# The order of the filler work and of four loads in the loop of a hybrid attention step

## The chip, the core and the metric

The program runs on one core of one Trainium2 chip. Its time is the device time of one execution in microseconds (us); the lower, the better. A core has TensorE (matrix products, rows PE and, for the loading of weights, PEld), VectorE (DVE), ScalarE (ACT), GpSimd (POOL) and SyncE (SP). In this program all transfers are issued by SyncE, in the order in which they were written down.

## What is computed

One layer of a decoder with two attention mixers side by side, for 2048 prompt positions and 8 sample tokens, in 32-bit floats:

```python
h = einsum('bsd,de->bse', x, w_in)            # 1024 -> qA,kA,vA,gA, qB,kB,vB,gB
# mixer A: 8 heads, three banded patterns with strides 1, 4, 16, merged by their maxima and denominators
# mixer B: 8 query heads on 2 key/value heads, one banded pattern, a learned sink per head
mix = concatenate([oa * silu(ga), ob * silu(gb)], axis=-1)     # 512 + 512 = 1024 rows
out = einsum('bse,ed->bsd', mix, w_o)                          # 1024 x 1024
y = layer_norm(ALPHA * x + out)
```

Every band has 128 positions behind each query and is worked in blocks of 128 queries with 128 or 256 keys. The keys and values are outputs as well.

## The kernel before

**Stages.** Four stages follow one another: the projection of keys, queries and some of the rest (0 to 240 us in the profile); the projection of values, with mixer A's sample tokens woven in (to 380 us); the attention loop (380 to about 1045 us); the output projection with the layer norm (to the end). A product of two 32-bit matrices is made of three products of split operands (high by high, high by low, low by high), so each weight tile is first split: VectorE copies it rounded ("h", L137), GpSimd subtracts to get the rest ("l", L138).

**The attention loop** (from L1113) runs over 16 jobs of 4 groups, 64 rounds, and two more rounds in which the last groups drain. A job is a head pair with one stride: rounds 0 to 47 are mixer A's four pairs with strides 16, 4 and 1; rounds 48 to 63 are mixer B's four pairs, four rounds each (rounds 48, 52, 56, 60). In a round TensorE computes scores of the new group (L823), turns the exponentials of the group before (transposes, L853) and multiplies the turned ones of the group before that with the values (L874). VectorE adds the mask and finds the extremes (L831), and copies the turned tiles out of PSUM (L859); ScalarE takes exponentials (L834). `fetch_q` (L800) reorders on VectorE the queries of the next group. A round has four steps; all engines execute in the order that is written (`manual_schedule`).

**Filler.** At each step `advance(RATE / 4)` lets a generator issue other products, charged with their columns divided by 2.4 per ns, until RATE / 4 = 3650 / 4 ns are spent; a yield of None ends the step. The filler is first `stream` (L568): the projection of 11 more tiles of 128 columns (three of B's queries, eight gates) in three passes of 4, 4 and 3 tiles; a pass goes over eight chunks of 256 positions, a tile and a chunk take 24 products (L628, tile `pg`), 2112 products in all. At the switch of passes the weights change: in the last chunk of a pass `Parts` puts four parts for each new tile in a list. `raw_step`, called at each step, loads parts into four buffers (`raw`, L142) and splits loaded parts, first in first out, two a step at most, if their tile has its place (`open`) and three steps have passed since the load was issued. A place can be opened only when the old tile in it is done; before the change `pend` opens it after the 24 products of the next tile.

**Head of the output projection.** After the stream, `out_weights` (L714) loads the last weights of the output projection (rows 2 and 3; rows 0 and 1 were put in the list in the last chunk, rows 5, 6, 4, 7 by `late_wo` in rounds 53, 57, 58, 59), waits until B's first two pairs are merged, and makes for three blocks of 128 positions the products with rows 0 to 5 of the eight row tiles (0 to 3 are mixer A's, 4 to 7 are B's four pairs): 3 x 6 x 2 x 3 = 108 products of 512 columns (L672). What is not done when the loop ends is issued right behind it.

**Merging.** When a pair of A is done, `merge_a` fetches weights F from DRAM for eight pieces (L1038), GpSimd multiplies and adds (L1050 to L1053), and the result goes to `ms`. `merge_b` does the like in three pieces (L951 to L997). These run in a queue of chains, one yield a step.

**Loads.** `loads` (L1084) issues the keys and queries of the next pair: for A in rounds 5 and 8 of a pair, for B in rounds 1 (keys) and 2 (queries) of the pair before.

**Last stage** (from L1161): first the sample tokens (L162), then the 16 blocks; a block that was begun in the loop lacks rows 6 and 7 (12 products), any other all eight (48 products).

Of the kernel before, what the change touches and what calls it, by code (L numbers as in the profile page):

```python
# [36 lines left out]
RATE = 3650  # L37
# [6 lines left out]
AHEAD = 3  # L44
# [7 lines left out]
def hymba_step(ctx, tc, xt, xs, xr, wq, wv, wo, tab, msk, ident, diag, sinks, lng, lnb,  # L52
# [513 lines left out]
    def stream(passes):  # L566

        with tc.tile_pool(name="gw", bufs=1, side="right", reuse_waits="tile") as gw, \  # L568
# [25 lines left out]
            def first_wo(i):  # L594
                t = kept.tile([128, 2, 8, 128], F32R, name="wo%d" % i, tag="w%d" % i)
                wo_parts[i].open((t[:, 0], t[:, 1]))

            nxt, pend = X5, []
# [4 lines left out]
            for pi, names in enumerate(passes):  # L603
# [7 lines left out]
                for c, c2 in zip(route, route[1:] + [None]):  # L611
                    c0 = 256 * c
                    n = TOK - c0 if c == 7 else 256
                    x, nxt = nxt, []
                    if c2 is None:
                        for name in more:
                            ws[name] = Parts(wq[TILES.index(name)])
                        if not more:
                            wo_parts.update((i, Parts(wo[:, i].rearrange("p (a b) -> p a b", b=128))) for i in range(2))
                    for i, name in enumerate(names):  # L620
                        p = ps.tile([128, 512], F32, name="pg", tag="mm", bufs=2)
                        wh, wl = ws[name]
                        for kt in range(8):
                            if c2 is not None and kt % 2 == 0 and i == 1:
                                nxt.append(piece(c2, len(nxt)))
                            xh, xl = x[kt // 2]
                            for e, (a, b) in enumerate(((wh, xh), (wh, xl), (wl, xh))):
                                T.matmul(p[:, :n], a[:, kt, :], b[:, kt % 2, :n], start=kt + e == 0, stop=kt == 7 and e == 2)  # L628
                                yield n / 2.4
                        EMIT[name[0]](go, XC, p[:, :n], name, c0, n)  # L630
                        if name[0] == "Q":
                            queries.append(name)
                        if news:
                            next(news, None)
                        for fn in pend:
                            fn()
                        pend = []
                        if c2 is None:
                            if not more and i < 2:
                                pend.append(lambda i=i: first_wo(i))  # L640
                            for e in range(i, len(more) if name == names[-1] else min(i + 1, len(more))):
                                pend.append(lambda e=e, name=more[e]: weights(e, name))
                nxt = x
            for fn in pend:
                fn()
# [6 lines left out]
    def mixed(pool, tb, kts, z, bufs, hbufs, here=None):  # L652

        nk = len(kts)
        h, l, t, g = [pool.tile([128, nk, 128], d, name="m" + a + z, bufs=n) for a, d, n in zip("hltg", (F32R, F32R, F32, F32), (hbufs, hbufs, bufs, bufs))]
# [48 lines left out]

    def late_wo(kt):

        pool, tag, bufs = {4: (ot, "oT2", 1), 5: (kp, "v", 2), 6: (kp, "k", 2), 7: (kp, "q", 2)}[kt]
        t = pool.tile([128, 2, 8, 128], F32R, name="wl%d" % kt, tag=tag, bufs=bufs)
        out_parts(kt, (t[:, 0], t[:, 1]))

    def out_weights():
        wO = wscope.enter_context(tc.tile_pool(name="wO", bufs=1, side="right", reuse_waits="tile"))
        for kt in (2, 3):
            out_parts(kt, [wO.tile([128, 8, 128], F32R, name="wo%d%s" % (kt, a)) for a in "hl"])  # L714
            yield None
            yield None
        while len(merged) < 2:
            yield None
        oh = wscope.enter_context(tc.tile_pool(name="oh", bufs=1, side="right", reuse_waits="tile"))
        xs_ = [oh.tile([128, D], F32, name="xh%d" % tb) for tb in range(AHEAD)]  # L720
        for tb, x in enumerate(xs_):
            dma(x, xr[tb * 128:tb * 128 + 128])
        kts = (0, 1, 2, 3, 5, 4)

        def gated(tb):
            cols = slice(tb * 128, tb * 128 + 128)
            t, g = [kept.tile([128, 6, 128], F32, name="h" + a, tag="p%d" % i) for i, a in enumerate("tg")]
            dma(g, gs[0:6, :, cols].rearrange("k p t -> p k t"))
            dma(t, ms[0:6, :, cols].rearrange("k p t -> p k t"))
            return t, g  # L730

        nxt = gated(0)
        first.clear()
        for tb, x in enumerate(xs_):
            t, g = nxt
            for _ in range(5 if tb == 0 else 3):
                yield None
            h, l = [oh.tile([128, 6, 128], F32R, name="h" + a, tag="h" + a) if tb % 2 else kept.tile([128, 6, 128], F32R, name="h" + a, tag="p%d" % (i + 2))
                    for i, a in enumerate("hl")]
            V.tensor_mul(t, t, g)  # L740
            split(h, l, t, V)
# [3 lines left out]
            for nh in range(2):  # L745
                p = ps.tile([128, 512], F32, name="po", tag="mm", bufs=2)
                yield from out_products(p, {kt: (h[:, kt], l[:, kt]) for kt in kts}, nh, True, True)
                xx = x[:, nh * 512:nh * 512 + 512]
                V.scalar_tensor_tensor(xx, xx, ALPHA, p, op0=OP.mult, op1=OP.add)
            first[tb] = x  # L750
# [334 lines left out]
    for before, p in zip(pairs, pairs[1:]):  # L1085
        s0 = starts[pairs.index(before)]
        loads[s0 + (1 if before.isb else 5)] = p, "k"
        loads[s0 + (2 if before.isb else 8)] = p, "q"
    spare = {starts[5] + 1: 5, starts[6] + 1: 6, starts[6] + 2: 4, starts[6] + 3: 7}
# [25 lines left out]
    with tc.manual_schedule(engines=set(ENGINES)):  # L1115
# [5 lines left out]
        for i in range(N + 2):  # L1121
# [16 lines left out]
            for sl in range(4):  # L1138
# [7 lines left out]
                advance(RATE / 4)  # L1146
# [16 lines left out]
    with tc.tile_pool(name="ol", bufs=1, reuse_waits="tile") as ol:  # L1163
# [7 lines left out]
        for i, tb in enumerate([16] + list(range(16))):  # L1171
# [3 lines left out]
            if tb in first:  # L1175
                x, m = first[tb], {}
# [5 lines left out]
            if tb < 16:  # L1182
                m.update(mixed(ol, tb, range(6, 8), "p", 2, 3, resident[-2:]))
# [151 lines left out]
```

## Time and profile before

| | us |
|---|---|
| median of 3 runs (lowest to highest) | 1236.95 (1236.46 to 1239.42) |
| the profiled execution: its own time | 1242.7 |
| the profiled execution: span from first to last instruction | 1240.9 |
| TensorE busy (matrix products) | 1149.8 |
| VectorE, ScalarE, GpSimd busy | 569.6, 430.5, 331.6 |
| mean granted TensorE clock | 0.972 |

Rows of the views by time read: start in us from the beginning of the span, duration, engine, line, operation, output<-inputs, shapes, count, and in square brackets how long the engine had been idle before and what released it. A view by windows gives for each stretch its length and then the busy time of PE, PEld, DVE, ACT and POOL with counts, the granted clock, the share of the DMA engines and GB/s. Products are pipelined: a row of n products lasts n spacings and a tail of some 0.2 us. A round begins where its sixteen score products (L823) begin.

### The profile page before, as it was taken

What the parts mean: (1) busy time and instruction counts of PE and PEld (TensorE: products, weight loads), DVE (VectorE), ACT (ScalarE), POOL (GpSimd) and SP (SyncE); (2) the same over time, 40 slices, a digit from 0 to 9 for tenths busy, and PEclk for the clock granted to TensorE, in tenths of its full rate; (3) what the DMA queues carried; (4) which work ended last, traced back from release to release, by engine and by line L of the source; (5) the groups of instructions that cost most, each with busy time, mean ns of one, the idle gap of its engine ahead of it and who ended that gap; (6) DMA issues with size and microseconds to landing.
All of it is one profiled execution on the core that took longest, in us unless ns stands there. A gap on an engine that the chain in (4) does not pass through costs nothing.

```text
span 1240.9 us, 23423 instructions
## 1 busy us (share of the span) xinstructions
PE 1149.8 (93%) x8614; PEld 1010.2 (81%) x8614; DVE 569.6 (46%) x1849; ACT 430.5 (35%) x1414; POOL 331.6 (27%) x400
## 2 busy tenths in 40 slices
PE   7999999999998999997999999699887977999997
PEld 7899999979978888986888788678766855688885
DVE  6522001010024554555665455555555775575544
ACT  3200111101103555554555455345443542132221
POOL 2233102120011000054224204620252332265442
PEclk9999999999999999998999999899998988999999
DMA  8745887293785654676458857676666755935531
GB/s 277 248 134 176 259 270 252 80 284 116 231 253 168 191 161 154 153 186 173 153 159 199 258 146 195 139 193 185 166 171 192 229 182 151 252 106 186 194 131 68
DMA packets 205971, 230.15 MB, mean 185 GB/s; under 512 B 34544, under 2 KB 174480, under 8 KB 205472
## 3 DMA queue, kind: packets, MB, share of 16 engines
q1 hardware_dynamic: 205856, 228.66, 63.2%
q8 instruction: 67, 1.10, 0.4%
q14 instruction: 48, 0.39, 0.1%
HBM read 158.52 MB, written 70.07 MB: 184 GB/s over the span
## 4 chain that ended last, share of the span: by engine, by line
PE 67%; DMA 16%; DVE 6%; ACT 5%; issue 3%; SPq 2%; POOL 1%; DVEq 0%; POOLq 0%; ACTq 0%
PE po L672 14%; PE pg L628 11%; PE pv L527 8%; DMA F<-fd 6%; PE ps_s L823 6%; PE ps_pt L853 5%; PE ppt L152 5%; PE pmm L152 5%; PE ps L152 5%; PE ps_o L874 4%; ACT pe L834 4%; PE po L152 3%; DVE pT L859 2%; DMA gx<-xd 2%; DMA raw<-in_wq 1%
## 5 line engine op out<-in xcount | busy, mean ns | idle before, releaser
L834 ACT ACTIVATE pe<-sm,st 128x256 f32<-128x256 f32 (+1 forms) x512 | 235.6, 461 | 228.1 <-DVE st L831 227.2
L831 DVE CUSTOM_DVE_ANT_0 sm<-ps_s,mk 128x256 f32<-128x256 f32 (+1 forms) x512 | 180.4, 375 | 139.5 <-PE ps_s L823 128.8
L853 PE MATMUL ps_pt<-idt,pe 128*128 128x128 f32 x848 | 141.2, 288 | 51.7 <-DVE pT L859 51.4
L628 PE MATMUL pg<-gx,gw 128*128 128x256 f32 (+1 forms) x1104 | 165.3, 293 | 8.3 <-DMA gx<-xd 2.9
L853 PEld LDWEIGHTS ps_pt<-idt,pe 128*128 128x128 f32 x848 | 94.0, 143 | 74.4 <-DVE pT L859 60.5
L628 PEld LDWEIGHTS pg<-gx,gw 128*128 128x128 f32 x1104 | 142.2, 192 | 9.7 <-issue 4.5
L859 DVE COPY pT<-ps_pt 128x512 f32<-128x512 f32 x176 | 121.2, 689 | 29.0 <-PE ps_pt L853 26.2
L1050 POOL TENSOR_TENSOR oT<-oT,F 128x256 f32<-128x256 f32 x32 | 23.5, 736 | 355.2 <-DMA F<-fd 256.8
L874 PE MATMUL ps_o<-pT,v 128*64 128x128 f32 (+1 forms) x1120 | 107.8, 337 | 0.0
L874 PEld LDWEIGHTS ps_o<-pT,v 128*64 128x64 f32 x1120 | 70.6, 138 | 40.3 <-issue 17.9
L834 ACT ACTIVATION_READ_ACCUMULATOR pe<-sm,st 128x1 f32 x512 | 95.8, 187 | 0.0
L823 PE MATMUL ps_s<-k,qo 64*128 64x256 f32 (+1 forms) x768 | 95.1, 389 | 0.0
L823 PEld LDWEIGHTS ps_s<-k,qo 64*128 64x128 f32 x768 | 68.9, 194 | 13.6 <-issue 2.2
L628 PE MATMUL pg<-gx,gw2h 128*128 128x256 f32 (+1 forms) x368 | 75.5, 293 | 1.2 <-ACT spe L406 1.2
L527 PE MATMUL pv<-wvh,xl 128*128 128x384 f32 (+1 forms) x224 | 70.3, 314 | 0.0
L527 PE MATMUL pv<-wvh,xh 128*128 128x384 f32 (+1 forms) x224 | 70.2, 313 | 0.0
L527 PE MATMUL pv<-wvl,xh 128*128 128x384 f32 (+1 forms) x224 | 70.1, 313 | 0.0
L628 PEld LDWEIGHTS pg<-gx,gw2h 128*128 128x128 f32 x368 | 58.8, 192 | 1.6 <-ACT spe L406 1.5
L628 PE MATMUL pg<-gx,gw2l 128*128 128x256 f32 (+1 forms) x184 | 54.1, 294 | 0.0
L539 ACT ACTIVATE vf<-pv 128x384 f32<-128x384 f32 (+1 forms) x32 | 14.0, 437 | 113.3 <-PE pv L527 67.3
L857 ACT ACTIVATE pT<-ps_pt 128x256 f32<-128x256 f32 (+1 forms) x48 | 23.6, 491 | 81.7 <-PE ps_pt L853 81.6
L628 PE MATMUL pg<-gx,gw3h 128*128 128x256 f32 (+1 forms) x240 | 49.9, 296 | 0.0
(278 smaller groups left out, 2485.7 us busy)
## 6 DMA issues: line engine op xcount, KB each, us to landing
gx<-xd SPq DMA_DIRECT2D x80, 512.0 KB
F<-fd SPq DMA_DIRECT2D x80, 192.0 KB
gs<-th SPq DMA_DIRECT2D x64, 128.0 KB
v<-vs SPq DMA_DIRECT2D x28, 256.0 KB
xo<-in_xr SPq DMA_DIRECT2D x13, 512.0 KB
xd<-xh SPq DMA_DIRECT2D x12, 512.0 KB
xd<-xl SPq DMA_DIRECT2D x12, 512.0 KB
kc<-in_kca SPq DMA_DIRECT2D x8, 768.0 KB
```

The costliest lines, as they stand in the source:

```text
L152: T.matmul(p[:, :n], a[:, kt, :], b, start=k == 0, stop=k == 23)
L527: T.matmul(p[:, :w], l, r[:, kt, :w], start=k == 0, stop=k == 23)
L628: T.matmul(p[:, :n], a[:, kt, :], b[:, kt % 2, :n], start=kt + e == 0, stop=kt == 7 and e == 2)
L672: T.matmul(p, a, b[:, nh * 4:nh * 4 + 4].rearrange("p a b -> p (a b)"), start=first and k == 0, stop=last and k == end)
L823: T.matmul(s[:, h, n % 4, :w], self.Q[g][r, n % 4 * 128:n % 4 * 128 + 128], self.keys(n)[r], start=True, stop=True)
L831: V.tensor_tensor_reduce(sm[:, :w], self.s[:, h, n % 4, :w], mk[:, MI[self.d], 256 - w:], -0.125, 3.0e38, op0=OP.add, op1=OP.min, accum_out=m)
L834: S.activation(p[:, :w], sm[:, :w], AF.Exp, scale=-1.0, bias=m, accum_out=den)
L853: T.transpose(pt[:, h, j], self.P[h, n][:, a:a + 128], idt)
L857: S.activation(t, pt, AF.Copy)
L859: V.tensor_copy(t, pt)
L874: T.matmul(o[64 * h:64 * h + 64, a:a + 128 * len(ns)], v[:, cv, kv:kv + 64], t[:, h, j:j + len(ns)].rearrange("p a b -> p (a b)"), start=n ...
L1050: G.tensor_mul(m, m, F[:, 0])
```

## The change

Nothing is computed otherwise; the order is changed in six places.

- `RATE` falls from 3650 to 3480; in round 0 each step gets `RATE / 2` in place of a quarter.
- The places of new weights are opened one step after the last product that used them (`soon(..., 1)`), no more after the next tile.
- In the loop, the head of the output projection covers four blocks. It begins with rows 0 to 3 for a block with an odd number, or while fewer than two pairs of B are merged; else with rows 0 to 5. The wait for B's first two merges is gone. The first block's inputs are loaded when the last chunk of the stream begins.
- The output weights change places: rows 0, 1, 2, 3 come in rounds 53, 57, 58, 59 (`late_wo`), rows 4 and 5 into the places of the first two gate tiles, rows 6 and 7 at the end of the stream.
- In the last stage a block that was begun with four rows makes up rows 4 and 5; the loads of all blocks' mixed and gate rows go to the places `p0` to `p3`, which the head's tiles also use.
- B's keys are issued in round 0 of the pair before and its queries in round 1.

```diff
-RATE = 3650
+RATE = 3480
-AHEAD = 3
+AHEAD = 4
...
                         if not more:
-                            wo_parts.update((i, Parts(wo[:, i]...)) for i in range(2))
+                            head.append(gated(0))
+                            wo_parts.update((i, Parts(wo[:, i]...)) for i in (4, 5))
...
-                        for fn in pend:
-                            fn()
-                        pend = []
                         if c2 is None:
                             if not more and i < 2:
-                                pend.append(lambda i=i: first_wo(i))
+                                soon(lambda i=i: first_wo(i), 1)
                             for e in range(i, len(more) if name == names[-1] else min(i + 1, len(more))):
-                                pend.append(lambda e=e, name=more[e]: weights(e, name))
+                                soon(lambda e=e, name=more[e]: weights(e, name), 1)
...
+    def gated(tb):
+        n = 6 if len(merged) > 1 and tb % 2 == 0 else 4
+        cols = slice(tb * 128, tb * 128 + 128)
+        t, g = [kept.tile([128, 6, 128], F32, name="h" + a, tag="p%d" % i)[:, :n] for i, a in enumerate("tg")]
+        dma(g, gs[0:n, :, cols].rearrange("k p t -> p k t"))
+        dma(t, ms[0:n, :, cols].rearrange("k p t -> p k t"))
+        return t, g
...
     def late_wo(kt):
-        pool, tag, bufs = {4: (ot, "oT2", 1), 5: (kp, "v", 2), 6: (kp, "k", 2), 7: (kp, "q", 2)}[kt]
+        pool, tag, bufs = {2: (ot, "oT2", 1), 0: (kp, "v", 2), 1: (kp, "k", 2), 3: (kp, "q", 2)}[kt]
...
     def out_weights():
-        for kt in (2, 3):
+        for kt in (6, 7):
             out_parts(kt, [wO.tile([128, 8, 128], F32R, name="wo%d%s" % (kt, a)) for a in "hl"])
             yield None
             yield None
-        while len(merged) < 2:
-            yield None
...
-        nxt = gated(0)
+        nxt = head[0]
         for tb, x in enumerate(xs_):
             t, g = nxt
-            for _ in range(5 if tb == 0 else 3):
+            dma(x, xr[tb * 128:tb * 128 + 128])
+            for _ in range(3 if tb else 1):
                 yield None
...
-        loads[s0 + (1 if before.isb else 5)] = p, "k"
-        loads[s0 + (2 if before.isb else 8)] = p, "q"
-    spare = {starts[5] + 1: 5, starts[6] + 1: 6, starts[6] + 2: 4, starts[6] + 3: 7}
+        loads[s0 + (0 if before.isb else 5)] = p, "k"
+        loads[s0 + (1 if before.isb else 8)] = p, "q"
+    spare = {starts[5] + 1: 0, starts[6] + 1: 1, starts[6] + 2: 2, starts[6] + 3: 3}
...
-                advance(RATE / 4)
+                advance(RATE / 4 if i else RATE / 2)
...
             if tb in first:
-                x, m = first[tb], {}
+                x, n = first[tb]
+                m = mixed(ol, tb, range(n, 6), "o", 2, 2) if n < 6 else {}
...
-                m.update(mixed(ol, tb, range(6, 8), "p", 2, 3, resident[-2:]))
+                m.update(mixed(ol, tb, range(6, 8), "p", 2, 4, resident[-2:]))
```

## What was predicted

> **What bounds the kernel now.** I read the page first, then the busy times by windows. TensorE is busy 93% of the span, so only the rest can be won, and the question is where it lies. One window of the loop in full flow, five others:
>
> ```profile
> 440.00:460.00 20.00, 20.00 (x177) 17.04 (x174) 12.28 (x51) 11.83 (x44) 0.00 (x0) 1.00 0.60 161
> 800.00:820.00 20.00, 13.41 (x93) 11.11 (x95) 10.04 (x33) 5.96 (x21) 11.62 (x19) 0.77 0.57 152
> 920.00:940.00 20.00, 10.86 (x87) 9.47 (x87) 6.18 (x23) 5.62 (x19) 7.61 (x11) 0.83 0.96 243
> 1000.00:1020.00 20.00, 12.64 (x97) 9.86 (x95) 18.09 (x52) 9.64 (x34) 10.68 (x12) 0.85 0.51 165
> 1020.00:1040.00 20.00, 15.64 (x86) 10.06 (x87) 11.01 (x30) 6.67 (x20) 6.88 (x8) 0.76 0.85 240
> 1100.00:1120.00 20.00, 20.00 (x88) 16.24 (x87) 13.25 (x18) 5.34 (x10) 14.04 (x11) 1.00 0.44 150
> ```
>
> At 440 and in the last stage (1100) TensorE has no gap. At 800 and 920 it stands for 7 and 9 us with the clock down, at 1000 VectorE is full (18.09) and TensorE waits, at 1020 it is idle again and slow. The waits, longest first, say what it waits for in the loop:
>
> ```profile
> PE ps_pt L853 <- DVE pT L859: 50.5, 33, 9.1
> ```
>
> Turns wait for VectorE's copies. VectorE executes in order, so the question of each such wait is what stood ahead of the copy. So I read VectorE's and SyncE's timelines at the three bad places.
>
> **The change, part by part.** I number rounds as the kernel part does.
>
> *B's queries one round earlier.* The 9.1 us wait, by the timelines of DVE, PE and SP:
>
> ```profile
> 934.97 0.43 DVE L800 COPY qo<-q 128x512 f32<-128x512 f32 x1 [9.50 <-DMA q<-qb]
> ```
> ```profile
> 936.06 1.11 PE L853 MATMUL ps_pt<-idt,pe 128*128 128x128 f32 x4 [9.14 <-DVE pT L859]
> ```
> ```profile
> 908.66 5.53 SPq L463 DMA_DIRECT2D od<-vsd  x8
> ...
> 920.11 1.35 SPq L906 DMA_DIRECT2D q<-qb  x2
> ```
>
> This is round 55, where `fetch_q` wants B's third pair. Its queries were issued in round 54 (its second step belongs here too: each load is two steps of two DMAs), 920 on SyncE, behind eight small loads of the sample tokens (5.53 us) and the merge's F. They land 15 us later. A round is some 10.5 us (below), so issued in round 53 they stand ahead of those eight loads and land about 10 us before they are needed: the whole 9.14 goes. What is late next is the same queue's F and `gx` (stream) traffic, at a DMA share of 0.96; so I bound the gain from 3 us (that traffic gives most of it back) to 11 (with the slow clock behind the wait, 0.83) and take 9.5. B's other loads (the keys' four DMAs and the other pairs' queries) move past F, `ms` and `raw` issues too; none of them shows a wait, nor do their buffers, whose last reader is a round back: nothing.
>
> *RATE.* The filler costs per product, and a round of B costs, by the chain of work:
>
> ```profile
> 499.04 2.02 PE pg L628 x17
> ...
> 964.34 1.95 PE ps_s L823 x16
> ...
> 974.85 1.95 PE ps_s L823 x16
> ```
>
> 0.119 us a product, 10.5 us a round. The stream is 2112 products charged 226.2 us; at 3.65 a round it ends after 62.0 rounds. At 3.48, with round 0 counted twice, after 64.0. So 65 products (7.0 / 0.107) pass from the rounds before 62 into rounds 62 and 63: 7.7 us leave the earlier part where TensorE is full. Late rounds have small gaps of their own, so I take 6.5 (3 to 7.7).
>
> Round 0 itself gains 30 products in this gap:
>
> ```profile
> 389.35 2.08 PE L823 MATMUL ps_s<-k,q 64*128 64x128 f32 x16 [3.43 <-DVE st L831]
> ```
>
> But the third tile's weights are then needed in round 0 and the fourth's early in round 1, before their splits; they are forced. I take nothing beyond their 3.6 us of work (plus or minus 1.5).
>
> *The end of the loop.* PE's timeline, then DVE's:
>
> ```profile
> 1006.16 2.00 PE L823 MATMUL ps_s<-k,qo 64*128 64x256 f32 x16
> ...
> 1017.72 1.11 PE L853 MATMUL ps_pt<-idt,pe 128*128 128x128 f32 x4 [3.79 <-DVE pT L859]
> 1019.58 0.39 PE L963 MATMUL pst<-idt,wts 128*32 128x128 f32 x1 [0.75 <-ACT pT L857]
> 1019.91 3.79 PE L823 MATMUL ps_s<-k,qo 64*128 64x256 f32 x16
> ...
> 1027.17 0.66 PE L853 MATMUL ps_pt<-idt,pe 128*128 128x128 f32 x4 [0.78 <-DVE pT L859]
> ...
> 1053.47 0.73 PE L672 MATMUL po<-wo,hh 128*128 128x512 f32 x2 [2.52 <-ACT hh L109]
> ...
> 1072.42 0.62 PE L162 MATMUL po<-wo,mixS 128*32 128x512 f32 x1
> ```
> ```profile
> 1004.82 2.20 DVE L137 CAST wo<-raw 128x256 fp32r<-128x256 f32 x2
> ```
>
> Round 62 takes 13.75 us without one filler product, because VectorE splits the four weights that the head needs first. From its start to the sample tokens (1072.42) it is 66.3. After: rows 0 to 3 come by `late_wo` and are split by round 60; the other sixteen parts follow in rounds 62 to 65, as many casts as before, but no head product waits for them before the third block. Rounds 62 and 63 with filler at 10.8 each (0.3 for casts): 21.6. Round 64 has neither filler nor scores: values 1.9 and five turns of 0.66 + 0.78, some casts between: 9.5. Three more for the first block's split (2.52 and its product's start). Then 108 products of the head at 20 / 88 = 0.227: 24.5; it is 108 as before, 4 + 4 + 6 + 4 rows in place of three times 6. Two gaps where a block's split waits for the loads before it: 3 (one is here, 2.52) and 2. Slow clock: 1.5. Sum 65.1 against 66.3: 1.2 gained, while 65 products more are done in it. The round of 64 is my weakest number; the tail can gain 8 (no gaps, full clock) or lose 6 (waits for `raw` as in 1004.82).
>
> On the clock: the scores at 1019.91 take 3.79, those at 1006.16 take 2.00, after a wait of 3.79. The Trainium skill, "TensorE: Matmul & The Clock Gate", Part 1, says that an idle window of some 3.4 us halves the clock until TensorE has been busy as long; the trace agrees, 3.79 against 2.00. By that rule the new tail, with gaps of 0.8 and 2.5, would not slow down at all, and the sum would be 1.5 lower; I keep the 1.5, as the window at 1020 has 0.76.
>
> *Places opened at once.* This speaks against the change. At the first switch of passes, DVE and SP:
>
> ```profile
> 562.29 0.69 DVE L859 COPY pT<-ps_pt 128x512 f32<-128x512 f32 x1
> ...
> 575.71 0.58 DVE L137 CAST gw<-raw 128x256 fp32r<-128x256 f32 x1 [5.56 <-DMA raw<-in_wq]
> ...
> 584.14 0.65 DVE L137 CAST gw<-raw 128x256 fp32r<-128x256 f32 x2 [3.20 <-DMA raw<-in_wq]
> ```
> ```profile
> 569.59 2.00 SPq L142 DMA_DIRECT2D raw<-in_wq  x4
> ```
>
> The first cast stands in round 21, step 0, and waits 5.56 for a part that SyncE could issue only at 569.59, behind the merge's F. When that part lands doesn't depend on the place. A pass of four tiles is charged 82.2 us and so ends at round 22.5 (82.2 / 3.65), after the change at 22.6; its last chunk begins four tiles (10.3 us charged) earlier, at 19.7 in both. The place was opened after two of these tiles, 1.4 rounds on, in round 21; now it is opened after one tile and a step, in round 20, step 1, and the cast stands in step 2: right behind the copy of 562.29, so VectorE waits from about 563 rather than 570.15 and holds its copies, the turns and TensorE 7.2 us longer. The second wait (3.20) then goes, as its part lands meanwhile. So 4 lost (0 to 7.2). At the second switch (DVE, POOL, SP):
>
> ```profile
> 802.73 1.30 DVE L137 CAST gw<-raw 128x256 fp32r<-128x256 f32 x2 [7.25 <-POOL F L1052]
> ```
> ```profile
> 804.63 2.79 POOL L138 TENSOR_TENSOR gw<-raw,gw 128x256 fp32r<-128x256 f32 x4
> ```
> ```profile
> 799.81 6.59 SPq L142 DMA_DIRECT2D raw<-in_wq  x4
> ```
>
> Here the next part waits for a buffer that GpSimd frees only behind the merge of A's third pair. By the same counting the lower RATE puts this switch 1.25 rounds later (45.1 to 46.3). The opening at once takes back most of that: the casts that wait here stood in step 1 of round 44 and now stand in step 3, half a round in which the stall is shorter. But the first tile's subtractions now queue behind the merge's last piece on GpSimd and no more before it, so the buffers come free later. I get 0.5 lost (3 gained to 9 lost).
>
> *Last stage.* Three blocks of 24 products and one of 12 in place of three of 12 and one of 48: 84 either way, then twelve of 48. Their loads wait for places that the head still holds, covered by the fourth block and the sample tokens (5.5 + 7 us): nothing; without that cover 3.
>
> **Sum.** -9.5 - 6.5 - 1.2 + 4 + 0.5 = -12.7, on the profile's span 1240.9: 1228.2. That execution took 1242.7, its median sisters 1236.95; I take the same difference from the median: 1224. What I call no change is within 0.3% (3.7 us), about what a measurement of this kernel can tell.
>
> **Rivals.**
> 1. *The tail closes up.* The tail gains 8, the queries 11, the first switch loses 2: -23, so 1214. For it: the window at 1020 is idle and slow; against: round 64 has nothing to fill its turns. 14%.
> 2. *The queue is the limit.* The queries' stall comes back as waits for F and `gx` (gain 3), and the first switch loses 6: -4.2, so 1233. For it: share 0.96; against: SyncE's 5.53 us now come after the queries. 13%.
> 3. *Slower: casts that stand too early.* At both switches VectorE waits from half a round earlier: 7.2 and 9 lost, with 1.8 of slow scores each; and since these waits end at times that the merges set, the 3 us saved in the rounds just before vanish: -14 + 18 = +4, so 1241. It decides from 14 us lost at the switches. For it: the 5.56 and 7.25 above; against: the part's landing after that serves more casts at once. 10%.
> 4. *No effect*: the loop is bound by the merges' chain of loads throughout. Against: the gapless window at 440. 2%.
>
> **How the numbers follow.** The forecast has 61%, its own range 1215 to 1231. Over 0.3% faster: 61 + 14 + half of rival 2 = 81%; same: the other half and rival 4, 9%; slower 10%. The range from 1211 to 1235 takes in rivals 1 and 2 and leaves out rival 3 and some of the edges.
>
> **What would show it.** No `qo` copy of round 55 waits for `q`; round 55 takes some 11 us. Round 62 holds 33 stream products and takes under 12. Before the first cast of the first switch VectorE waits 10 us or more, in round 20. Head products start with `wo0` right after round 65 begins, with 41 of 108 in the loop's steps, counted as above. I am wrong if the window around round 55 stays as idle as 10.86 of 20, if the switches cost over 14 us more, or if the last stage no longer runs gapless.

## The result, and the profile after

The changed kernel is slower: 1244.12 us median of 5 runs (1241.27 to 1245.74) against 1236.46 (1232.59 to 1239.42) of the kernel before beside it, ratio 1.0066 with a 95% interval of 1.0040 to 1.0093. Its profiled execution took 1243.91 us, span 1242.1. The forecast was 1224, with a range of 1211 to 1235 and 10% on slower.

The profiled execution of before on which the prediction rests was long in its span (1240.9). The kernel before was therefore profiled once more among the experiments: 1236.17 us, span 1234.4. This span and that of the profile after differ by 7.7 us, the two medians by the same, so this second profile of before is the one to set against the profile after. The two profiles of the kernel before differ by 1.3 to 1.6 us in each of the first four stretches below; differences of that size between single profiles say nothing.

I cut both spans where the score products (L823) of a round begin. The rows below are from the view by windows: stretch, length, then busy time of PE, PEld, DVE, ACT, POOL, granted clock, share of the DMA engines, GB/s. The stretches are rounds 21 and 22 (the first switch of passes), 34 and 35, 44 to 46 (the second switch), 54 to 56 (B's third queries), and round 62 to the sample tokens' products (L162). The last stage, from there to the start of its last product, took 159.5 us before and 159.7 after, with TensorE busy all the time. First the kernel before, run again:

```profile
564.61:592.40 27.79, 21.29 (x164) 17.94 (x164) 15.93 (x54) 11.08 (x39) 14.51 (x21) 0.94 0.71 182
693.38:714.85 21.47, 19.92 (x170) 16.90 (x169) 11.35 (x42) 11.19 (x39) 0.00 (x0) 1.00 0.77 243
784.33:824.14 39.81, 30.55 (x242) 25.69 (x241) 21.42 (x75) 16.18 (x58) 16.69 (x29) 0.91 0.72 182
901.97:946.56 44.59, 32.42 (x258) 27.64 (x257) 20.92 (x80) 17.04 (x59) 19.56 (x28) 0.89 0.72 191
999.58:1065.89 66.31, 52.80 (x267) 37.12 (x266) 40.10 (x98) 17.77 (x49) 20.06 (x22) 0.85 0.69 205
```

The same rounds of the changed kernel:

```profile
563.67:599.71 36.04, 22.32 (x160) 18.50 (x159) 16.60 (x56) 11.30 (x39) 17.31 (x25) 0.81 0.63 150
699.24:726.06 26.82, 22.82 (x167) 18.66 (x166) 11.16 (x41) 11.28 (x39) 2.52 (x4) 0.87 0.81 263
795.59:839.58 43.99, 31.83 (x237) 26.18 (x236) 22.21 (x77) 16.39 (x58) 21.72 (x34) 0.88 0.61 155
915.47:948.09 32.62, 30.17 (x267) 25.28 (x266) 21.00 (x79) 16.84 (x59) 16.89 (x25) 1.00 0.71 193
1003.05:1073.37 70.32, 57.81 (x331) 44.20 (x330) 41.03 (x112) 18.79 (x54) 20.92 (x24) 0.90 0.69 205
```

So rounds 54 to 56 win 12.0 us, with the clock full and TensorE busy for 30.2 of 32.6 us; the first switch loses 8.25, rounds 34 and 35 lose 5.35, the second switch 4.2, the end 4.0; the last stage is the same. All other rounds from 0 to 61 together win 2.6 (482.7 against 485.3). The sum is +7.2. Of the 12.0 us, 1.95 come back within that 2.6: rounds 57 to 61 take 55.0 us instead of 53.0, since a wait for the sample tokens' work, 2.3 us in rounds 54 to 56 before, now stands there with 1.4.

The list of TensorE's waits in the changed kernel (total, times, longest) is to be set against 50.6 us, 38 times, longest 8.8, in the kernel before, run again (the 50.5 us that the prediction began with are for the span from 500 us on):

```profile
PE ps_pt L853 <- DVE pT L859: 37.6, 38, 7.2
PE ps_pt L853 <- DVE stT L930: 10.2, 1, 10.2
```

Together 47.8 us, no more than before: by this list alone the change looks harmless. On the two pages TensorE is busy for 1146.8 of 1234.4 us (before, run again) and for 1149.4 of 1242.1 (after), so it stands 5.1 us longer and works 2.6 longer on the same products, at a lower clock in places. The lengths of the rounds tell where.

**The first switch.** VectorE's and SyncE's timelines of the changed kernel, the stretch between the last copy of round 20 and the turns behind it:

```profile
561.51 0.68 DVE L859 COPY pT<-ps_pt 128x512 f32<-128x512 f32 x1
575.37 1.96 DVE L137 CAST gw<-raw 128x256 fp32r<-128x256 f32 x4 [13.18 <-DMA raw<-in_wq]
...
585.23 0.64 DVE L137 CAST gw<-raw 128x256 fp32r<-128x256 f32 x2 [2.55 <-DMA raw<-in_wq]
```
```profile
569.46 1.89 SPq L142 DMA_DIRECT2D raw<-in_wq  x4
```

The parts are issued at 569.46, as before (569.59), and the cast ends its wait at 575.37, as before (575.71; 575.09 in the profile run again). Only the waiting begins earlier: the cast now stands directly behind the copy of 561.51, and VectorE does nothing for 13.18 us, where it did half a round of work before and then waited 5.56 (4.86 in the profile run again). TensorE's timeline shows who pays:

```profile
577.58 1.12 PE L853 MATMUL ps_pt<-idt,pe 128*128 128x128 f32 x4 [10.25 <-DVE stT L930]
```

**B's queries.** The timelines of VectorE and SyncE in the changed kernel, rounds 53 to 55:

```profile
922.34 0.64 DVE L800 COPY qo<-q 128x512 f32<-128x512 f32 x1
```
```profile
913.38 1.86 SPq L906 DMA_DIRECT2D q<-qb  x2
...
918.32 0.34 SPq L581 DMA_DIRECT2D gx<-xd  x1
...
933.06 6.50 SPq L463 DMA_DIRECT2D od<-vsd  x8
```

No copy of queries waits any more, neither this one nor the next at 934.73. Two things have moved: the queries are issued a round earlier, and the eight loads of the sample tokens (`od`), which stood ahead of the queries and of the stream's `gx`, now stand behind both. The second is the work of RATE: these loads are listed with the stream's tiles, and on SyncE they come behind `gx` in the kernels with RATE 3480 and ahead of it in those with 3650.

**The end.** TensorE's and VectorE's timelines of the changed kernel behind the loop:

```profile
1034.56 1.22 PE L672 MATMUL po<-wl,hh 128*128 128x512 f32 x2 [2.33 <-ACT hh L109]
...
1043.98 0.37 PE L963 MATMUL pst<-idt,wts 128*32 128x128 f32 x1 [4.65 <-DVE wts L959]
...
1050.69 0.73 PE L672 MATMUL po<-wl,hh 128*128 128x512 f32 x2 [2.04 <-ACT hh L109]
```
```profile
1037.49 0.29 DVE L137 CAST wo7h<-raw 128x256 fp32r<-128x256 f32 x1 [2.26 <-DMA raw<-in_wo]
...
1041.21 0.69 DVE L137 CAST wo7h<-raw 128x256 fp32r<-128x256 f32 x2 [2.45 <-DMA raw<-in_wo]
```

Two waits of VectorE for output weights 7, which only the last stage reads, stand ahead of the last steps of pair 7's statistics (`wts`); the transpose of these (L963) stands ahead of the head's next products on TensorE.

### The profile page after: what moved, and what is told of

Read it like the earlier page. It is cut to its first block, busy times and chain, and to the rows that moved or that the text cites. A ratio compares the mean times of both kernels' runs of the same rounds, so it can differ in the third digit from the quotient of the medians.

```text
span 1242.1 us, 23436 instructions
## 1 busy us (share of the span) xinstructions
PE 1149.4 (93%) x8614; PEld 1006.3 (81%) x8614; DVE 566.0 (46%) x1855; ACT 430.9 (35%) x1417; POOL 328.6 (26%) x402
## 4 chain that ended last, share of the span: by engine, by line
PE 65%; DMA 13%; DVE 7%; ACT 5%; issue 4%; POOL 3%; SPq 2%; POOLq 0%; DVEq 0%; ACTq 0%
PE po L672 13%; PE pg L629 11%; PE ps_s L823 7%; PE pv L527 7%; PE ps_pt L853 5%; PE pmm L152 5%; PE ps L152 5%; PE ppt L152 4%; ACT pe L834 4%; PE ps_o L874 4%; DMA F<-fd 4%; PE po L152 3%; DVE pT L859 3%; DVE sm L831 2%; DMA k<-ks 2%
## 5 line engine op out<-in xcount | busy, mean ns | idle before, releaser
L853 PEld LDWEIGHTS ps_pt<-idt,pe 128*128 128x128 f32 x848 | 90.7, 141 | 73.3 <-DVE pT L859 48.9
L823 PE MATMUL ps_s<-k,qo 64*128 64x256 f32 (+1 forms) x768 | 95.5, 390 | 0.0
L823 PEld LDWEIGHTS ps_s<-k,qo 64*128 64x128 f32 x768 | 69.3, 195 | 13.4 <-issue 1.8
L527 PE MATMUL pv<-wvl,xh 128*128 128x384 f32 (+1 forms) x224 | 69.4, 310 | 0.0
L672 PE MATMUL po<-wl,mho 128*128 128x512 f32 x192 | 59.7, 392 | 0.0
L172 DVE SCALAR_TENSOR_TENSOR th<-th,pg 128x256 f32<-128x256 f32 (+1 forms) x64 | 26.9, 420 | 48.7 <-ACT th L168 48.3
```

Of the source, the lines that this page charges most:

```text
L172: V.scalar_tensor_tensor(th[:, :n], th[:, :n], 1.0, p, op0=OP.add, op1=OP.mult)
L527: T.matmul(p[:, :w], l, r[:, kt, :w], start=k == 0, stop=k == 23)
L672: T.matmul(p, a, b[:, nh * 4:nh * 4 + 4].rearrange("p a b -> p (a b)"), start=first and k == 0, stop=last and k == end)
L823: T.matmul(s[:, h, n % 4, :w], self.Q[g][r, n % 4 * 128:n % 4 * 128 + 128], self.keys(n)[r], start=True, stop=True)
L853: T.transpose(pt[:, h, j], self.P[h, n][:, a:a + 128], idt)
```

## The experiments

The lengths of the same rounds in all profiles, and the ratios to before of the same job (the letters of the theories are defined anew in each expectation). The lengths are of one profile each, in us:

| kernel | 21, 22 | 34, 35 | 44-46 | 54-56 | 0-61 | 62 to sample | ratio (95%) |
|---|---|---|---|---|---|---|---|
| before (b0) | 27.8 | 21.5 | 39.8 | 44.6 | 619.0 | 66.3 | 0.9989 (0.9962-1.0016) |
| loads | 28.0 | 21.5 | 42.8 | 44.9 | 623.3 | 66.2 | 0.9987 (0.9960-1.0014) |
| RATE | 29.1 | 27.0 | 37.3 | 41.5 | 618.9 | 75.2 | 1.0065 (1.0039-1.0091) |
| places | 35.8 | 21.5 | 41.1 | 44.9 | 629.0 | 68.7 | 1.0061 (1.0031-1.0090) |
| head | 27.6 | 21.5 | 40.9 | 43.5 | 619.9 | 67.1 | 1.0015 (0.9994-1.0036) |
| head, loads | 27.9 | 21.5 | 39.6 | 44.7 | 620.1 | 67.6 | 1.0013 (0.9996-1.0031) |
| head, loads, RATE | 28.4 | 26.2 | 37.4 | 32.6 | 609.2 | 71.8 | 0.9964 (0.9942-0.9985) |
| all four (after) | 36.0 | 26.8 | 44.0 | 32.6 | 622.2 | 70.3 | 1.0066 (1.0040-1.0093) |
| head, RATE, places | 34.2 | 26.0 | 44.6 | 38.5 | 628.1 | 70.8 | 1.0131 (1.0098-1.0164) |
| head, loads, places | 33.1 | 21.5 | 40.7 | 43.5 | 627.4 | 63.5 | 1.0037 (1.0015-1.0060) |

**1. The kernel before, unchanged.**

> The kernel before, unchanged. Theory A (the profiled execution of before, 1242.7 us, was an unusual one, 6 us over the median, because its transfers fell badly): round 55 takes clearly less than the 20.5 us of that profile, and the span is some 1235 us. Theory B (the profile is typical and only the profiling adds time): round 55 takes about 20 us again and the span is about 1240 us.

1236.01 us; round 55 takes 20.2 us in this profile too, as theory B had it, and yet the span is 1234.4, as theory A had it. So the stall of the queries was there in both profiles, and it is not what made the first one long: its 6.5 us more are spread over many rounds.

**2. The loads alone** (before, with `0 if before.isb` and `1 if before.isb` in `loads`).

> The kernel before with B's keys and queries issued one round earlier, nothing else. Theory A (the stall of round 55 is there in few executions): within 3 us of before. Theory B (it is there in each): 9 to 13 us faster. In both, VectorE no longer waits for q in round 55.

1236.12 us, no difference: the time of theory A, but not its reason, as the stall is there again in experiment 1. The wait for `q` is gone, and yet rounds 54 to 56 take 44.9. TensorE waits 5.5 us for `gx` there, and works 35.2 us where it worked 32.4, at a granted clock of 0.85. TensorE's and SyncE's timelines say why:

```profile
928.88 1.65 PE L628 MATMUL pg<-gx,gw 128*128 128x256 f32 x6 [3.34 <-DMA gx<-xd]
```
```profile
908.26 6.05 SPq L463 DMA_DIRECT2D od<-vsd  x8
...
922.09 2.16 SPq L581 DMA_DIRECT2D gx<-xd  x1
```

The stream's next chunk `gx` stood behind the same eight loads and the merge's F. The queries had hidden that it was late as well.

**3. RATE alone** (3480, and round 0 twice).

> The kernel before with RATE 3480 and the doubled first round, nothing else. Theory A (products moved from full rounds to the idle end are won): 4 to 8 us faster. Theory B (they are paid again behind the loop, where the head now starts later): no change, within 3 us.

1245.15 us, slower by itself, which neither theory had. To round 61 it is level (618.9); the end takes 8.9 us longer. TensorE's and VectorE's timelines there:

```profile
1042.43 0.37 PE L963 MATMUL pst<-idt,wts 128*32 128x128 f32 x1 [14.80 <-DVE wts L959]
```
```profile
1039.72 0.64 DVE L137 CAST wo3h<-raw 128x256 fp32r<-128x256 f32 x2 [8.27 <-DMA raw<-in_wo]
```

The stream ends two rounds later, so the head's weights are loaded two rounds later, and their casts come to stand ahead of pair 7's statistics.

**4. The places alone** (`soon(..., 1)` for `pend`).

> The kernel before with the weights' places opened one step after their last use, nothing else. Theory A (the cast stands half a round earlier before a part whose landing the merge sets): 4 to 7 us slower at the first switch of passes, and at the second switch up to 5 us either way. Theory B (the places opened early spread the casts): 1 to 4 us faster.

1245.10 us, slower, and by a little more than theory A had. The first switch takes 35.8 instead of 27.8, the second little more than before. VectorE's timeline:

```profile
573.05 1.96 DVE L137 CAST gw<-raw 128x256 fp32r<-128x256 f32 x4 [11.99 <-DMA raw<-in_wq]
```

**5. The head alone** (all of the change but RATE, places and loads).

> The kernel before with the first part alone: four head blocks that begin with mixer A's rows, weights 4 and 5 first, the blocks' loads early; RATE 3650, the step by step opening and the loads' places of before. Theory A (the loss is in the other parts' collisions and in weights 6 and 7): the loop is as before to round 61 within 1 us a round, the head's products begin 2 to 6 us earlier than 17.3 us after round 63, round 63 to the sample tokens takes 46 to 52 instead of 52.6, and the time is 1230 to 1236, ratio 0.995 to 1.000. Rival (this part brings the loss behind the loop by itself: weights 7's casts stand ahead of pair 7's statistics here as well): round 63 to the sample tokens takes 55 to 60, and the time is 1239 to 1244, ratio 1.002 to 1.006.

1237.45 us, between the two readings: no difference that can be told, and the expected gain at the end is not there. The first head product does come earlier (22.4 us after round 62 began, against 31.0), but the sample tokens do not (67.1 against 66.3): the third block waits for its rows, whose product with the gates stands on VectorE behind pair 7's merge (TensorE, then VectorE):

```profile
1054.45 2.07 PE L677 MATMUL po<-wl,hh 128*128 128x512 f32 x4 [5.28 <-ACT hh L109]
```
```profile
1051.69 0.96 DVE L995 TENSOR_TENSOR oT<-oT,F 128x768 f32<-128x768 f32 x1 [1.80 <-DMA F<-fd]
1052.57 0.95 DVE L745 TENSOR_TENSOR ht<-ht,hg 128x768 f32<-128x768 f32 x1
```

**6. Head and loads.**

> The kernel before with the head's part and mixer B's loads moved up, RATE 3650 and the step by step opening kept: what the step by step kernel (0.9964) has without its RATE part. Theory A (the moved loads gain only where the gx pieces of the stream do not fall into the same round, which RATE 3480 brings): rounds 55 and 56 take 32 to 34 us, TensorE waits there for gx, and the time is that of the head's part alone, 1235 to 1239, ratio 0.999 to 1.003. Rival (the loads gain by themselves, and RATE is what loses at the end): rounds 55 and 56 take 22 to 24 us and the time is 1225 to 1229, ratio 0.990 to 0.994.

1238.28 us, as the theory had it: rounds 54 to 56 take 44.7. The stretch has only moved by a round, to 54 (15.87 us), so that 55 and 56 alone show 28.8, not the 32 to 34 expected.

**7. Head, loads and RATE**, that is the change without the places (`pend` kept).

> The changed kernel with the weights' places opened step by step again, as before; the other three parts stay. Theory A (the change's costs are waits for loads, where one part lets several transfers meet on SP's queue: each costs where it stands and is carried to the end): rounds 21 and 22 fall from 24.61 + 11.43 us to about the 18.95 + 10.14 of the kernel with the RATE part alone, rounds 44 and 45 from 33.5 to about 27, rounds 55 and 56 stay near 22, and the time falls by 7 to 13, to 1231 to 1237, ratio to before 0.996 to 1.000. Theory B (the stretch behind the loop sets the end, and what the loop wins or loses is given back there): the loop ends 7 to 13 us earlier, the first product of the head comes no earlier than 1030, and the time stays within 3 us of 1244, ratio 1.004 to 1.008.

1232.39 us, ratio 0.9964, faster than before, as theory A had it. The first switch falls to 28.4, the second to 37.4, 54 to 56 stay at 32.6. So the places cost 7.7 + 6.6 us here. VectorE's timeline at the first switch, to be read beside that of the changed kernel:

```profile
568.70 0.69 DVE L864 COPY pT<-ps_pt 128x512 f32<-128x512 f32 x1
574.86 0.33 DVE L137 CAST gw<-raw 128x256 fp32r<-128x256 f32 x1 [5.13 <-DMA raw<-in_wq]
```

**8. The change without the loads.**

> The changed kernel with mixer B's loads at their old places; the other three parts stay. Theory A: moving the loads gains only where the stream stands elsewhere, which the RATE part brings; so here, unlike in the kernel before, their return costs: rounds 55 and 56 go from 11.77 + 10.35 us back to about the 17.57 + 13.43 of the RATE part alone, and the time rises by some 9 us to 1253, ratio to before 1.011 to 1.015. Theory B: the 9 us lie in the loop and are made up behind it, where the head's products wait for their weights in any case: 1244 within 3 us. A third reading, that the loads' part does nothing at all, as in the kernel before (ratio 0.9987): rounds 55 and 56 stay within 2 us of 22.1.

1253.20 us (four runs only), by the ratios 0.65% more than the changed kernel, as theory A had it. Rounds 54 to 56 take 38.5 instead of 32.6. The loads' part, worth nothing in the kernel before, is worth some 6 to 9 us here. I had expected 55 and 56 to take 31 together; they took 28.0.

**9. The change without RATE.**

> The changed kernel with RATE 3650 and no doubled first round; head, places opened at once and loads moved up stay. Theory A (each part costs or gains where its loads meet others): rounds 21 and 22 take 34 to 37 us as in the kernel with the places alone (23.72 + 12.03), rounds 55 and 56 stay near 33, since the loads' gain needs the stream where RATE 3480 puts it, and the time is 1243 to 1249, ratio 1.005 to 1.010, no better than the changed kernel. Rival (RATE is the part that loses, as its run alone with 1.0065 says, and without it the others gain): 1233 to 1238, ratio 0.997 to 1.001.

1241.25 us, between the two readings and slower than before; the first switch takes 33.1, and 54 to 56 take 43.5 although the loads are moved (55 and 56 take 30.1, where 33 was expected). The time is below the 1243 expected, since the end takes only 63.5.

**10. Places opened at once, but later** (in the changed kernel):

```diff
-                                soon(lambda i=i: first_wo(i), 1)
+                                soon(lambda i=i: first_wo(i), 4)
...
-                                soon(lambda e=e, name=more[e]: weights(e, name), 1)
+                                soon(lambda e=e, name=more[e]: weights(e, name), 4)
```

> The changed kernel with the weights' places still opened all at once, but four steps (one round) after the last products that use the old weights are listed instead of one step. Theory A (what costs is the place of the first casts in VectorE's order: they stand ahead of a round's copies of pT and wait there for a load that lands at the same time either way): VectorE's wait of 13.18 us in the first switch falls below 6, rounds 21 and 22 go from 24.61 + 11.43 us to 28 to 30 together, rounds 44 and 45 from 33.5 to 27 to 29, and the time to 1230 to 1236, ratio 0.995 to 1.000, as with the step by step opening (0.9964). Rival (opening at once costs by itself: four casts in a row, and eight loads of weights that ask for the queue together): the two pairs of rounds stay at 33 and more each, time 1241 to 1247.

1230.62 us, ratio 0.9954 (0.9933 to 0.9974). The two switches in the view by windows, then VectorE at the first:

```profile
560.64:587.22 26.58, 20.95 (x161) 17.47 (x159) 15.48 (x52) 11.30 (x39) 13.48 (x20) 0.94 0.69 181
784.91:822.18 37.27, 30.06 (x238) 25.51 (x236) 23.40 (x77) 16.40 (x58) 18.52 (x30) 0.95 0.69 170
```
```profile
566.71 0.69 DVE L859 COPY pT<-ps_pt 128x512 f32<-128x512 f32 x1 [0.41 <-PE ps_pt L853]
571.61 0.34 DVE L137 CAST gw<-raw 128x256 fp32r<-128x256 f32 x1 [3.38 <-DMA raw<-in_wq]
```

All places are still opened together; only the cast has its place behind copies of the round again, two of them. Its part lands 10.9 us after round 21 begins, against 11.7 in the changed kernel. The whole loss of the places is gone (26.6 against 36.0, 37.3 against 44.0). At the second switch the wait moved on by a round, to 46, so rounds 44 and 45 alone (21.1) came out shorter than expected.

**11 to 13. Output weights 7 behind the first head block**, in the changed kernel (a_late7), in the kernel of experiment 7 (n_late7) and in that of experiment 10 (s4_late7):

```diff
-        for kt in (6, 7):
-            out_parts(kt, [wO.tile(...) for a in "hl"])
-            yield None
-            yield None
+        places = {kt: [wO.tile(...) for a in "hl"] for kt in (6, 7)}
+        out_parts(6, places[6])
+        for _ in range(4):
+            yield None
...
             first[tb] = x, n
+            if tb == 0:
+                out_parts(7, places[7])
```

> The changed kernel with one step moved: the load and the casts of output weights 7 (rows that only the last stage reads) are queued behind the first head block instead of ahead of it. Theory A: they are what VectorE holds ahead of pair 7's statistics, so TensorE's wait of 4.65 us before the transpose of the statistics (L963) goes, and with it the half clock behind it: the 108 head products go from 38.8 us to about 34, the stretch from round 63 to the sample tokens' products from 60.3 to about 54, and the time to 1237 to 1240, ratio 1.000 to 1.003. Rival: pair 7's statistics and the head's own loads (hg, ht, xh) are late by themselves: the casts go, the stretch stays at 58 to 62, and the time within 2 us of 1244; or the casts only come back in front of the sample tokens' products, with the same 4 to 6 us there.

1244.09 us, ratio 1.0061 (1.0035 to 1.0087): no gain in time. The wait of 4.65 us is gone, and the 108 head products take 34.9 us instead of 38.8, both as expected; from round 62 to the sample tokens it is 67.8 instead of 70.3, less of a gain than expected (from round 63 57.8, where 54 was expected). But rounds 0 to 61 took 623.8 in this profile, and the median shows nothing. The next wait stands at the third block, in TensorE's and VectorE's timelines:

```profile
1059.09 1.59 PE L672 MATMUL po<-wl,hh 128*128 128x512 f32 x4 [3.22 <-ACT hh L109]
```
```profile
1051.64 0.96 DVE L992 TENSOR_TENSOR oT<-oT,F 128x768 f32<-128x768 f32 x1 [1.14 <-DMA F<-fd]
...
1057.12 0.96 DVE L740 TENSOR_TENSOR ht<-ht,hg 128x768 f32<-128x768 f32 x1 [0.85 <-DMA ht<-ms]
```

> The kernel with the step by step opening and the three other parts, and with output weights 7 queued behind the first head block. Theory A: TensorE's wait of 3.14 us before pair 7's statistics transpose goes, round 63 to the sample tokens takes 57 to 59 us instead of 61.75, and the time is 1228 to 1231, ratio 0.992 to 0.996. Rival (as in the changed kernel with the same step: the wait goes, and the head's later blocks give the time back in waits for their own loads): 61 to 62 us, time within 1.5 us of 1232, ratio 0.995 to 0.998.

1230.05 us, ratio 0.9950 (0.9931 to 0.9969), 62 to sample 69.4 instead of 71.8: in the direction of the theory, but within the interval of experiment 7.

> The changed kernel with both steps moved: the weights' places opened all at once but four steps after the last products that use the old ones, and output weights 7 queued behind the first head block. Theory A (the casts ahead of pair 7's statistics cost where the head itself is next, so the two add): TensorE's wait of 2.40 us before the statistics transpose goes, round 63 to the sample tokens takes 57 to 59 us instead of 61.1, and the time is 1226 to 1230, ratio 0.991 to 0.995. Rival (as when the step was made in the changed kernel: the time returns in the later head blocks' waits for ht, which wait for pair 7's merge): 61 to 62 us, the time that of the four steps alone, 1230 to 1233, ratio 0.995 to 0.997.

1234.25 us, ratio 0.9983 (0.9963 to 1.0003), 62 to sample 71.9 instead of 71.2, and a wait of 2.96 us before the statistics that stays. No gain. What VectorE holds ahead of the statistics is now weights 6, which this kernel loads a round later than experiment 12 does. Its timeline:

```profile
1028.37 0.29 DVE L137 CAST wo6h<-raw 128x256 fp32r<-128x256 f32 x1 [1.76 <-DMA raw<-in_wo]
```

So the edit took one set of casts away and left its like, and no run moved both. What else sets the end when the stream ends at 64.0 is not settled; pair 7's merge, with its F ahead of the third block's rows, is what the timelines show next, and no run tried that.

## Why the prediction was wrong

Its five terms, against the second profile of before:

| term | predicted | measured |
|---|---|---|
| queries | -9.5 (-11 to -3) | -12.0 (rounds 54 to 56) |
| RATE | -6.5 (-7.7 to -3) | +2.7 (-2.6 in the quiet rounds, +5.35 in 34 and 35) |
| end of the loop and head | -1.2 (-8 to +6) | +4.0 |
| first switch | +4 (0 to 7.2) | +8.25 |
| second switch | +0.5 (-3 to +9) | +4.2 |
| sum | -12.7 | +7.2 |

The line of RATE holds every round that no other line names. Of the 19.9 us between the two sums it has 9.2, the two switches have 8.0, the end 5.2, and the queries take off 2.5.

**The step that turned the sign is the one on the places.** The prediction had the mechanism: where the cast stands, when its part lands, that VectorE holds its copies from about 563. It took the 7.2 us that follow as a bound and wrote 4, because "The second wait (3.20) then goes, as its part lands meanwhile". This clause failed. In rounds 21 and 22 TensorE stands 13.7 us instead of 6.5, all of the 7.2 more, and it works 1.0 longer, as some of the work behind the waits runs at half the clock. VectorE's second wait becomes shorter (2.55, against 4.51 in the profile of before, run again), but it stays: the next parts go into buffers that are free only when GpSimd has subtracted from the first ones, and that comes behind the last piece of the merge. GpSimd's timeline of the changed kernel:

```profile
578.68 2.80 POOL L138 TENSOR_TENSOR gw<-raw,gw 128x256 fp32r<-128x256 f32 x4
```

SyncE issues the next parts at 580.32, where it issued them before (580.30). At the second switch RATE's delay by itself is no loss but a gain of some 2.5 (experiments 3 and 7 against b0), and beside it the opening costs 6.6, where "0.5 lost" was written for both. VectorE's first wait there, in the changed kernel and then in that of experiment 7:

```profile
807.95 0.64 DVE L137 CAST gw<-raw 128x256 fp32r<-128x256 f32 x2 [7.25 <-DMA raw<-in_wq]
```
```profile
800.97 0.66 DVE L137 CAST gw<-raw 128x256 fp32r<-128x256 f32 x2 [5.38 <-DMA raw<-in_wq]
```

The waits end 12.4 and 13.0 us after round 44 begins, so here too the part lands no later and the wait begins earlier. TensorE stands 12.2 us in these three rounds instead of 7.4 and works 1.8 longer; this row explains only a part of it, and how the rest comes about is open. Without RATE the opening costs only 1.0 to 1.3 there (9 against 6, 4 against b0), but 5.2 to 8.0 at the first switch.

Together the places cost 14.2 us beside the three other parts; against the kernel before the two switches lose 12.4. That is about the 14 from which rival 3 was said to decide; it stood at 1241 and 10%. (Its sum counts the 1.8 us of slow scores once, though it says each; with both it is +5.6, or 1242.6.) Experiment 10 shows the cause directly: with the opening four steps later the loss is gone.

**Queries.** The size was nearly right, the reason half of it. "What is late next is the same queue's F and `gx` (stream) traffic" was put down as a bound and then not taken; alone, the loads do exactly that (experiment 2, rival 2). They gain only together with RATE, which moves the `od` loads from ahead of `gx` to behind it (experiments 6, 7, 8). That the order of these loads is the reason is read from SyncE's rows; no run moved the `od` loads alone.

**RATE.** "7.7 us leave the earlier part where TensorE is full" fell short: the rounds outside the named places win 2.6, that is 4.6 up to round 53 less the 1.95 of rounds 57 to 61. Beside head and loads RATE does take off about what was written for it, 0.49% or 6.1 us (experiment 7 against 6), but in rounds 54 to 56, so that this agreement is luck. And the shift of the stream makes a new meeting of loads, which no step looked for. TensorE's timeline of the changed kernel in rounds 34 and 35, and SyncE's:

```profile
711.26 2.07 PE L629 MATMUL pg<-gx,gw 128*128 128x256 f32 x8 [2.40 <-DMA gx<-xd]
713.26 3.79 PE L823 MATMUL ps_s<-k,qo 64*128 64x256 f32 x16
```
```profile
703.57 1.00 SPq L581 DMA_DIRECT2D gx<-xd  x2
...
705.14 4.47 SPq L940 DMA_DIRECT2D sd<-stT  x4
```

The chunk's loads now stand between those of queries (698.81 and 702.34 on SyncE) and the stores of statistics; before, SyncE issued them from 684.10 to 687.19, ahead of both. Seven of the eight profiles with RATE 3480 show the loss (26.0 to 27.8 us for the two rounds), one does not (a_late7, 21.5): there the order is the same, but the last two of these loads are issued 1.1 us after round 34 begins instead of 4.3. No run isolates this meeting. Round 0 was right: 3.55 us longer for 30 products more, won back over the next twenty rounds (170.8 against 175.6).

**The end.** Rounds 62 to 64 and the start of the head took 31.5 us where the steps sum to 34.1 (21.6 + 9.5 + 3). The head's 108 products took 38.8 where 24.5 + 5 + 1.5 = 31.0 was written: TensorE stood for 7.1 us of it, where 5 was written, and was at work for 31.7, where 24.5 + 1.5 was written. The term that failed most is "Slow clock: 1.5". The waits of 2.33 (ahead of the first product), 4.65 and 2.04 were each followed by some 3 us of work at half the clock.

**What was right.** No copy of round 55 waits; round 55 took 11.77 us; round 62 holds 32 stream products and took 10.02; VectorE waits 13.18 in front of the first cast, from round 20 on; the last stage is gapless. The head's first product came 4.3 us into round 65, where "right after" its beginning was written.

In short: head and loads bring nothing alone, RATE with them wins some 0.5%, the places lose 1%. The kernels of experiments 7, 10 and 12 (0.9964, 0.9954, 0.9950) are faster than both; between the three the intervals do not choose.

## What to carry to other kernels

On an engine that executes in the order written, giving an instruction leave to run earlier means that it waits earlier: ask when its input lands, and count all that is queued behind it. A wait that goes uncovers the next on the same queue, so before a load is moved, list what else it stood ahead of or behind. Edits to an order are not to be added up from runs of each alone: here the loads were worth nothing and RATE a loss by itself, and beside the head the two were a gain together.

## What the runs showed of the hardware

In all fifteen profiles TensorE's granted clock changes only on a grid of 3.41 us, between 1.00 and 0.50. TensorE's timeline of n_late7 shows what gaps do to it; the two rows are products of 512 columns before and after a gap of 2.04 us:

```profile
1025.71 0.62 PE L677 MATMUL po<-wl,hh 128*128 128x512 f32 x2
...
1028.61 1.22 PE L677 MATMUL po<-wl,hh 128*128 128x512 f32 x2 [2.04 <-ACT hh L109]
```

Two products pass in 1.22 instead of 0.62, and the half rate lasts to about 1032. In the changed kernel the wait of 2.40 us ahead of 711.26 doubled the scores of 713.26 as well (3.79 against 2.00). The length alone does not decide, though: in experiment 7 a gap of 3.14 us, before the transpose of pair 7's statistics, was followed by 2.8 us at the full rate, and only the next gap, again 2.04, by half. What decides in these traces is how long TensorE was busy within one stretch of the grid. The views by windows, taken at the grid (length, busy time of PE, granted clock, share of the DMA engines, GB/s), of n_late7 and then of the kernel of experiment 7:

```profile
1025.07:1028.48 3.41, 1.50 (x7) 1.00 0.87 246
1028.48:1031.90 3.42, 3.29 (x8) 0.50 0.96 253
```
```profile
1022.69:1026.11 3.42, 2.01 (x9) 1.00 1.01 381
1026.11:1029.52 3.41, 1.68 (x8) 1.00 1.05 338
1029.52:1032.93 3.41, 1.37 (x6) 1.00 0.35 75
1032.93:1036.35 3.42, 3.42 (x9) 0.50 1.01 278
```

The gap of 3.14 lies across two stretches, which keep 2.01 and 1.68 us of work, and the clock stays at 1.00; the next stretch has 1.37, and the one behind it runs at 0.50. From 375 to 1075 us in the fifteen profiles, 100 of 101 stretches at the full clock in which TensorE was busy for less than 45% were followed by half, 15 of 60 with 45 to 60%, and none of some 2700 with more.

The prediction used a rule of the Trainium skill, "TensorE: Matmul & The Clock Gate", Part 1, that an idle window of some 3.4 us halves the clock, and said that by it gaps of 0.8 and 2.5 would not slow the tail; it kept 1.5 us for slow clock all the same. The length of the stretch agrees, 3.41 us here; that all of it must be idle does not, as 1.50 us of work did not keep the clock. The prediction's own trace did not show it either: there the clock halves at 1013.88, when the wait of 3.79 begins, behind a stretch with waits of 1.42 and 0.78 and 1.26 us of work. So waits are to be priced together: what counts is how much of one such stretch they take.
